# Output stage of a pooling trunk: P7 of five blocks as seven leaf products in place, row stores issued from GpSimd, operand work reordered

## The chip, the cores and the metric

One core of a Trainium2 chip runs the whole kernel. The metric is device time in microseconds (us) of that core. The kernel before takes 909.25 us, the median of three runs (909.12 to 909.44); the execution that the profiler recorded took 909.13 us, with a span of 907.3 us from its first to its last instruction. TensorE (PE in the profile) multiplies, VectorE (DVE) and ScalarE (ACT) do elementwise work and read results out of PSUM, GpSimd (POOL) does small elementwise work and issues some DMAs, SyncE (SP) issues most DMAs.

## The reference, cut to what matters

With one layer, the trunk is one pooling mixer between two RMSNorms:

```python
normed = rms_norm(x, norm_w[0])
u, gate = split(normed @ in_w, 2)            # 4096 x 1024 each
pooled = trailing means of u (windows 2, 4, 8, 16) - u
y = (einsum(pooled, group_w) + group_b) * scale * silu(gate)
h = x + y @ out_w                            # 4096x1024 @ 1024x1024
out = rms_norm(h, final_norm_w)
```

Everything is float32. The change touches the last two lines: the output product, the residual and the last norm.

## The kernel before, in words

**Products.** All large products follow Strassen's scheme in Winograd's form: seven products P1 to P7 of half-size matrices in place of eight. Each factor is held as a high and a low part in a float32 format that TensorE multiplies fast, and each half-size matmul is three passes: high·high, high·low, low·high (`mm3`, L774).

**Stages.** `steps` (L1287) lists the work in order: stages `a` and `b`, the input projection for four blocks of 1024 rows each, and then the output stage `o` for eight blocks (`NBO`) of 512 rows, `b` = 0 to 7. Within a block of the output stage the order is `ORDER_OUT` = P1, P7, P6, P2, P5, P4, P3 (L33). The main loop (L1566) goes through the steps `n`. At step `n` it issues loads for output steps up to `n + 4` (`load_o`, L1068), operand splits for up to `n + 2` (`split_o`, L1082), and then the products of step `n` with their eviction (`run`, L1322).

**A product of the output stage.** A block has four operand quarters 11, 21, 12, 22 of y, read from DRAM (`load_y`). `split_o` forms the sum that product needs and splits it: ScalarE copies it to the high part, VectorE subtracts to get the low part. The parts go to one of four operand tiles `op`, taken in turn. `product_out` (L894) runs two row halves `j`, each of four contraction chunks of three passes, 24 matmuls of 512 columns in all. The eight PSUM banks of 512 columns are four pairs x, v, y, spare, whose places turn from block to block (`sets_of`, L1315). P1 goes to x, and ScalarE copies it to y, so that P6 accumulates on it; P7 goes to v, P2 to x, P5 and P3 to y, P4 to v.

**Inner products.** In blocks 2 to 7, P2 is itself done as seven products of quarter-size matrices (`split_inner`, `product_inner`), here called leaves: two contraction chunks of three passes, six matmuls of 256 columns each. P2, P3, P4, P1, P7 run at P2's place; P6 and P5 within product P5; `add_inner` adds cells of the spare banks into rows with VectorE. The leaves' weights are formed in block 1 by `form_inner` into four kept tiles. A similar scheme in place, with cells of a bank copied to others between leaves, exists in stage `b` for two blocks (`product_seven`, L713); the output stage does not use it.

**Rows.** Output rows are collected in row tiles `hs` (two halves of a block, two tiles of 128 rows each). ScalarE evicts P7, P6 and P2 into them, GpSimd's accumulating DMAs add x (`add_h`, L1059), VectorE adds P5, P4, P3. `finish` (L1116) then normalizes a half, after P4 for the first and after P3 for the second: two squares of 1024 on ScalarE with their sums, a root on ScalarE (`inverse`, `rsqrt`), a reciprocal on VectorE refined by four small GpSimd operations, two row multiplies on VectorE, and two stores that SP issues. The junk output of a square goes to a tile from the common store. The last block has code of its own at its end (`late_factor`, `late_scalar`, `late_vector`).

**Tiles.** Operands, weights before splitting, rows and junk share 11 tiles `st` and 8 tiles `vt` (`Slots`, `take`, `give`, `keep`).

**Order.** A scheduler orders the instructions of each engine; `tc.issue_after(i)` makes what is issued inside come after instruction `i` in that order. Each engine then executes its own queue in that order, waiting on semaphores.

## Time and profile before

| | |
|---|---|
| median of three runs | 909.25 us |
| profiled execution, its own time | 909.13 us |
| its span | 907.3 us |
| busy: TensorE, VectorE, ScalarE, GpSimd | 898.9, 731.5, 494.0, 83.9 us |
| granted TensorE clock, mean over the span | 0.997 |
| first and last leaf of the output stage start | 701.0 and 889.6 us |

In the views below, a row of a timeline is: start in us from the start of the span, duration in us, engine, line, operation, tiles written and read, shape, count, and in brackets the idle time before it and what ended that. A row of a group ends with count, then busy us and mean ns of one, then idle time before with what ended it. A row of waits is: who waited for whom, us in total, times, longest. A row of windows is: the stretch, its length, then for each engine busy us and count, the granted clock, the busy share of the DMA engines, GB/s. A row of DMA issues ends with KB and the median us from issue to landing. Matmuls are pipelined, so a matmul's own duration (275 to 379 ns) is longer than the distance between starts; the distances are what counts.

### The profile page before, as it was taken

Reading aid. Unit: us, or ns where it says so; the run is one execution under the profiler, and the core shown is the slowest. Engines: PE = TensorE matmul, PEld = TensorE weight load, DVE = VectorE, ACT = ScalarE, POOL = GpSimd, SP = SyncE. Lnnn points to the kernel's source line nnn. Section 1 sums busy time; section 2 is a strip of 40 time slices with the busy share of each in tenths; the row PEclk is TensorE's granted clock in tenths of the full one; section 3 lists DMA queues with packets and bytes.
Section 4 is the critical chain, followed back from the end, with each engine's and each line's share of the span. In section 5 each row is a group of like instructions: output and inputs, shape, how many; then the busy total and the mean of one; then the engine's idle time right before and its main releaser. Section 6 shows DMA issues by size and latency. Waiting matters only on the chain.

```text
span 907.3 us, 11824 instructions
## 1 busy us (share of the span) xinstructions
PE 898.9 (99%) x4392; PEld 790.2 (87%) x4392; DVE 731.5 (81%) x868; ACT 494.0 (54%) x760; POOL 83.9 (9%) x166
## 2 busy tenths in 40 slices
PE   9999999999999999999999999999999999999996
PEld 7888888888888888889889888888888898988986
DVE  3889896985995999798599499599759768868686
ACT  7869547447446565346545636545535435445434
POOL 0020100100110000000000000001122113112200
PEclk9999999999999999999999999999999999999998
DMA  9987667677575462323554475528585675775732
GB/s 341 401 303 238 251 229 229 215 270 251 224 267 198 161 217 85 110 100 116 206 189 148 176 267 168 192 70 232 173 232 172 171 192 158 169 220 162 175 140 92
DMA packets 71401, 179.41 MB, mean 198 GB/s; under 512 B 6576, under 2 KB 24624, under 8 KB 71344
## 3 DMA queue, kind: packets, MB, share of 16 engines
q1 hardware_dynamic: 58720, 146.13, 46.4%
q0 software_dynamic: 11904, 31.48, 13.5%
q10 hardware_dynamic: 720, 1.06, 0.3%
q8 instruction: 34, 0.56, 0.3%
q14 instruction: 23, 0.19, 0.1%
HBM read 117.81 MB, written 60.83 MB: 197 GB/s over the span
## 4 chain that ended last, share of the span: by engine, by line
PE 95%; DVE 2%; DMA 1%; ACT 1%; issue 0%; DVEq 0%; ACTq 0%
PE bank L779 89%; PE bank L879 3%; PE bank L725 2%; PE bank L421 1%; DMA st<-in_x 1%; DMA early<-in_wut 0%; ACT st L461 0%; DVE vt L1245 0%; ACT st L1152 0%; PE bank L487 0%; DVE vt L172 0%; DVE w L169 0%; ACT st L443 0%; ACT early L443 0%; DVE vt L1204 0%
## 5 line engine op out<-in xcount | busy, mean ns | idle before, releaser
L779 PE MATMUL bank<-op,w 128*128 128x512 f32 x2592 | 560.9, 379 | 0.0
L779 PEld LDWEIGHTS bank<-op,w 128*128 128x128 f32 x2592 | 489.4, 189 | 70.2 <-ACT vt L175 0.4
L779 PE MATMUL bank<-w,op 128*128 128x512 f32 (+1 forms) x1212 | 262.2, 377 | 0.0
L779 PEld LDWEIGHTS bank<-w,op 128*128 128x128 f32 x1212 | 226.0, 189 | 31.0
L169 DVE TENSOR_TENSOR op<-st,op 128x1024 fp32r<-128x1024 f32 x134 | 162.3, 1219 | 58.0 <-ACT op L175 57.6
L175 ACT ACTIVATE op<-st 128x1024 fp32r<-128x1024 f32 x134 | 140.2, 1052 | 113.4 <-PE bank L779 64.5
L175 ACT ACTIVATE vt<-bank 128x512 f32<-128x512 f32 (+1 forms) x115 | 65.8, 590 | 46.5 <-PE bank L779 43.1
L169 DVE TENSOR_TENSOR st<-st,st 128x1024 f32<-128x1024 f32 (+1 forms) x42 | 45.8, 1104 | 18.9 <-ACT st L256 16.8
L169 DVE TENSOR_TENSOR op<-vt,op 128x1024 fp32r<-128x1024 f32 x42 | 51.1, 1219 | 8.1 <-ACT op L175 8.1
L175 ACT ACTIVATE op<-vt 128x1024 fp32r<-128x1024 f32 x42 | 44.1, 1054 | 24.9 <-PE bank L779 20.9
L1062 POOL DMA_DIRECT2D st<-in_x x19 | 16.8, 893 | 387.0 <-DVE op L169 352.9
L175 ACT ACTIVATE st<-bank 128x512 f32<-128x512 f32 (+1 forms) x61 | 34.7, 585 | 30.6 <-PE bank L779 19.1
L175 ACT ACTIVATE bank<-bank 128x512 f32<-128x512 f32 (+1 forms) x60 | 32.1, 537 | 30.1 <-PE bank L779 26.0
L933 DVE TENSOR_TENSOR_SCAN vt<-vt,window 128x1040 f32<-128x1040 f32 x16 | 37.9, 2376 | 1.6 <-DMA yd<-vt 1.5
L169 DVE TENSOR_TENSOR w<-st,w 128x1024 fp32r<-128x1024 f32 (+1 forms) x26 | 30.8, 1198 | 9.2 <-ACT w L175 9.2
L175 ACT ACTIVATE w<-st 128x1024 fp32r<-128x1024 f32 (+1 forms) x26 | 26.6, 1035 | 17.4 <-PE bank L779 9.5
L175 ACT ACTIVATE vt<-tails 128x32 f32<-128x32 f32 x28 | 6.3, 228 | 46.8 <-DVE vt L933 25.7
L979 DVE SCALAR_TENSOR_TENSOR vt<-vt,vt 128x1024 f32<-128x1024 f32 x24 | 29.3, 1219 | 0.3
L172 DVE TENSOR_TENSOR st<-st,vt 128x1024 f32<-128x1024 f32 x22 | 26.1, 1215 | 3.4 <-DMA vt<-rd 3.4
L1125 DVE SCALAR_TENSOR_TENSOR vt<-vt,ors,st 128x1024 f32<-128x1024 f32 x18 | 22.5, 1282 | 7.6 <-POOL ors L235 7.6
L1245 DVE TENSOR_TENSOR st<-bank,st 128x512 f32<-128x512 f32 x23 | 15.8, 689 | 14.0 <-PE bank L779 14.0
L984 DVE SCALAR_TENSOR_TENSOR st<-vt,colt,st 128x512 f32<-128x512 f32 x38 | 26.8, 743 | 0.1
(143 smaller groups left out, 735.3 us busy)
## 6 DMA issues: line engine op xcount, KB each, us to landing
st<-in_xt SPq DMA_DIRECT2D x28, 512.0 KB, 6.3
sd<-st POOLq DMA_DIRECT2D x28, 512.0 KB, 4.0
st<-sd SPq DMA_DIRECT2D x26, 512.0 KB, 4.2
st<-in_x SPq DMA_DIRECT2D x20, 512.0 KB, 6.0
st<-yd SPq DMA_DIRECT2D x20, 512.0 KB, 4.6
yd<-st SPq DMA_DIRECT2D x19, 512.0 KB, 3.1
out<-vt SPq DMA_DIRECT2D x18, 512.0 KB, 4.6
st<-wod SPq DMA_DIRECT2D x15, 512.0 KB, 4.0
```

The lines of the kernel that those rows point to most:

```text
L169: return nc.vector.tensor_tensor(out=dst, in0=a, in1=b, op=ALU.subtract)
L172: nc.vector.tensor_tensor(out=dst, in0=a, in1=b, op=ALU.mult)
L175: return nc.scalar.activation(dst, src, func)
L725: latest[0] = nc.tensor.matmul(cell(n, c).rearrange("p (a s) -> p a s", s=2), x1, x2, start=i == P1 and k + m == 0, stop=k == 1 and m == 2 ...
L779: latest[0] = nc.tensor.matmul(ps, a, b, start=start and n == 0, stop=stop and n == 2, skip_group_check=True).ins
L879: latest[0] = nc.tensor.matmul(ps, x1, x2, start=i in (P1, P7) and k + n == 0, stop=k == 1 and n == 2, skip_group_check=True,).ins
L933: nc.vector.tensor_tensor_scan(out=sums_[:, HIST:], data0=flat[:, HIST:], data1=flat[:, HIST - win : 2 * end - win], initial=first_sum, op ...
L979: nc.vector.scalar_tensor_tensor(out=s[:, :, at : at + H], in0=s[:, :, at : at + H], scalar=1.0 / win, in1=v[:, :, HIST:], op0=ALU.mult, o ...
L984: nc.vector.scalar_tensor_tensor(out=sg[:, j], in0=s[:, j, at : at + H], scalar=bias_c[2 * grp + j], in1=sg[:, j], op0=ALU.add, op1=ALU.mult,)
L1062: nc.gpsimd.dma_start(out=hs[b][half, j][:, n], in_=x[row_of(b, half, j), n * H : (n + 1) * H], accum_op=ALU.add,)
L1125: nc.vector.scalar_tensor_tensor(out=us[j], in0=us[j], scalar=rs[:, j : j + 1], in1=fw[0], op0=ALU.mult, op1=ALU.mult,)
L1245: partial["added"] = nc.vector.tensor_tensor(out=dst, in0=src, in1=dst, op=ALU.add).ins
```

## The change

- Blocks from 3 on (`OWN` = 3, five blocks) do P7 as seven leaves in place in the pair v. The first two leaves (P1 and P5) are put into the last quarter of product P1 (`own_first`); the others are put around P6's first row half, of which six matmuls each stand between leaves (`own_rest`). Four copies of 256 columns on ScalarE (`own_move`) take cells of the banks to other cells or to a row tile between leaves, and one VectorE add completes the second bank.
- The operand of P7 is split as P2's is: four narrow sums of 256 columns, and two operand tiles (`split_own`).
- The weights of the leaves are formed in block 1 for P2 and in block 2 for P7 (`load_inner`, `sum_inner`, `split_weight`), with three kept tiles each. Sums are formed in place in the loaded tiles.
- P2's leaves at its place run in the order P2, P4, P1, P3, P7, and the split of its four sums is issued later than that of its plain quarters (`late_split`).
- `finish` squares the two halves of a row apart (512 each), with the junk output in a PSUM bank, and GpSimd adds the two sums before the root. Row multiplies and stores of a block's first half are issued after the narrow sums of the next block's P7, where that is done by leaves (`late_rows`). Stores are issued by GpSimd.
- Row tiles are taken when P1 and P2 of the block run, not four steps ahead (blocks 0 to 6).
- Operand work of step `n + 2` is ordered behind the reading out of the products of step `n - 2` (`read_out`).

```diff
+OWN = 3
...
+    def load_inner(i):
+        raws[i] = {"held": [take() for _ in range(2)]}
+        for h, u in enumerate(raws[i]["held"]):
+            nc.sync.dma_start(out=u, in_=wod[i][h])
+
+    def sum_inner(i):
+        us = raws[i]["held"]
+        b11, b12 = (quarter(us[0], j) for j in range(2))
+        b21, b22 = (quarter(us[1], j) for j in range(2))
+        if i == P7:
+            sub(b12, b11, b12)
+            sub(b22, b22, b12)
+            add(b11, b22, b11)
+            sub(b21, b21, b22)
...
+    def split_weight(i, *ps):
+        for p in ps:
...
+            copy(home[0], raws[i][p])
+            sub(home[1], raws[i][p], home[0].bitcast(F32))
...
+    def split_own(u):
+        at = u.rearrange("p (g k) (j c) -> p g j k c", g=2, j=2)
+        b11, b12, b21, b22 = (at[:, g, j] for g in range(2) for j in range(2))
+        v = take("p (n k c) -> p n k c", n=4, k=2)
+        sub(v[:, 0], b12, b11)
+        sub(v[:, 1], b22, v[:, 0])
+        sub(v[:, 2], b22, b12)
+        row_sums[0] = sub(v[:, 3], b21, v[:, 1]).ins
+        plain_op = next_op("p (s g k j c) -> p s g j k c", s=2, g=2, k=2, j=2)
+        split(plain_op.rearrange("p s g j k c -> p s (g k) (j c)"), u)
+        sums_op = next_op("p (s n k c) -> p s n k c", s=2, n=4, k=2)
+        split(sums_op, v)
...
+    def own_move(dst, src):
+        with tc.issue_after(own.get("moved", latest_copy[0])):
+            own["moved"] = copy(own["m5"] if dst is None else own_cell(dst), own_cell(src)).ins
+
+    def own_first(t, b, sets):
+        own.clear()
+        own.update(t=t, v=sets["v"])
+        own_into(P1, 1, True)
+        own_into(P5, 3)
...
+        own_move(0, 1)
+        own_move(None, 3)
+
+    def own_rest(piece):
+        own_into(P2, 0)
+        own_into(P6, 1)
+        own_move(2, 1)
+        piece(0)
+        own_into(P7, 2)
+        own_into(P3, 1)
+        own_move(3, 2)
+        piece(1)
+        own_into(P4, 2)
+        bank = own["v"][1].rearrange("p (j b) -> p j b", j=2)
+        add(bank, bank, own["m5"].unsqueeze(1).to_broadcast([P, 2, 256]))
...
-            for p in (P2, P3, P4, P1, P7):
+            for p in (P2, P4, P1, P3, P7):
                 product_inner(p)
...
-    def finish(b, half):
+    def finish(b, half, sets):
+        parts = small.tile([P, 2, 2], F32, tag="parts", name=f"parts{b}_{half}")
...
-            junk = take("p (a b) -> p a b", a=2)
-            nc.scalar.activation(junk, us[j], AF.Square, accum_out=ss[:, j : j + 1])
-            give(junk)
+            for n in range(2):
+                nc.scalar.activation(
+                    sets["v" if half else "y"][j], us[j][:, n], AF.Square,
+                    accum_out=parts[:, n, j : j + 1],
+                )
+        nc.gpsimd.tensor_tensor(out=ss, in0=parts[:, 0], in1=parts[:, 1], op=ALU.add)
         rs = inverse(b, half, ss)
+        if half and b + 1 >= OWN:
+            late_rows.append(lambda: norm_rows(b, half, us, rs))
+        else:
+            norm_rows(b, half, us, rs)
...
-            nc.sync.dma_start(
+            nc.gpsimd.dma_start(
                 out=out[row_of(b, half, j), :], in_=us[j].rearrange("p a b -> p (a b)")
             )
...
+        if kind == "o" and b < NBO - 1 and i in (P1, P2):
+            load_h(b, int(i == P1))
+        if kind == "o" and b >= OWN and i == P1:
+            t = split_up.pop(n)
+            out_part(P1, t, sets["x"][0], 0, range(4))
+            out_part(P1, t, sets["x"][1], 1, range(2))
+            own_first(split_up.pop(n + 1), b, sets)
+            with tc.issue_after(latest[0]):
+                out_part(P1, t, sets["x"][1], 1, range(2, 4))
+            evict_o(b, i, sets)
...
+        (1, P1): lambda: load_inner(P2),
+        (1, P6): lambda: sum_inner(P2),
+        (1, P5): lambda: split_weight(P2, P7, P6),
+        (1, P4): lambda: (split_weight(P2, P5, P4), end_weights(P2)),
+        (2, P1): lambda: load_inner(P7),
+        (2, P6): lambda: sum_inner(P7),
+        (2, P5): lambda: split_weight(P7, P7, P6),
+        (2, P4): lambda: (split_weight(P7, P5, P3), end_weights(P7)),
...
-        advance("split", n, split_step, split_reach)
...
+        if kind == "o" and i == P6 and late_split:
+            with tc.issue_after(own["moved"]) if own else nullcontext():
+                late_split.pop()()
+        with ExitStack() as order:
+            for ins in read_out.get(n - 2, {}).values():
+                order.enter_context(tc.issue_after(ins))
+            advance("split", n, split_step, split_reach)
+        for f in late_rows:
+            with tc.issue_after(row_sums[0]):
+                f()
+        late_rows.clear()
```

200 lines of the change are left out of this document (122 added, 78 removed).

## The prediction

> **What bounds the kernel now.** I read the page first (busy shares, the chain that ended last), then TensorE in order of time over two blocks of the output stage, then what TensorE ever waited for.
>
> ```profile
> span 907.3 us, 11824 instructions
> ...
> PE 95%; DVE 2%; DMA 1%; ACT 1%; issue 0%; DVEq 0%; ACTq 0%
> ```
> ```profile
> 710.89 26.07 PE L779 MATMUL bank<-w,op 128*128 128x512 f32 x120
> 736.79 1.50 PE L879 MATMUL bank<-w,op 128*128 128x256 f32 x12
> 738.13 0.83 PE L879 MATMUL bank<-inner,op 128*128 128x256 f32 x6
> 738.80 0.83 PE L879 MATMUL bank<-w,op 128*128 128x256 f32 x6
> ...
> 740.14 2.75 PE L779 MATMUL bank<-w,op 128*128 128x512 f32 x12
> ...
> 746.66 13.55 PE L779 MATMUL bank<-w,op 128*128 128x512 f32 x62
> ```
> ```profile
> PE bank L1374 <- PEq L1685: 0.8, 1, 0.8
> PE bank L421 <- DMA early<-in_group_w: 0.4, 1, 0.4
> ```
>
> TensorE holds 95% of the chain, and its only two waits lie in the first microseconds. Starts give the prices: 120 matmuls of 512 columns take 736.79 − 710.89 = 25.90 us, 215.8 ns each; thirty leaf matmuls of 256 columns take 740.14 − 736.79 = 3.35 us, 111.7 ns each; a leaf of six takes 0.67. So a plain output product (24 × 215.8) costs 5.18 us and seven leaves (42 × 111.7) cost 4.69. A block of six plain products and one of leaves is 6 × 5.18 + 4.69 = 35.77 us without a gap. Only two things can move the end: less work on TensorE, or a wait put in front of it.
>
> **The change on TensorE.** In blocks 3 to 7, P7 becomes seven leaves: 5 × (5.18 − 4.69) = 2.45 us less. That is the whole gain, 0.27%. P2's leaves only change order, and everything up to the output stage keeps its order on each engine.
>
> The Trainium skill ("TensorE: Matmul & The Clock Gate", Back-to-back issue gap) gives N/2.4 + 2.5 ns for one matmul after another; 512 columns agree with the 215.8, 256 columns would be 109.2 against the measured 111.7, and the gain by it would be 2.97 us. The same section's sustained figure of about 131 ns for 512 columns is not what this trace shows; the row decides.
>
> ```profile
> L175 ACT ACTIVATE op<-st 128x1024 fp32r<-128x1024 f32 x43 | 45.1, 1056 | 64.5 <-PE bank L779 40.5 <-DVE st L169 10.8 <-PE bank L879 7.8
> ```
>
> **The work added, and its cover.** Per block from 3 on: one more operand split of 1024 (ScalarE 1.06, VectorE 1.22 us), four narrow sums instead of none (0.42 each), four bank moves of 256 columns, one add of 512 (0.69, as a bank add below); and everywhere eight squares of 512 into a PSUM bank in place of four of 1024, and a GpSimd add in front of each root.
>
> ```profile
> 720.70:756.50 35.80, 35.80 (x188) 31.94 (x187) 24.09 (x32) 15.85 (x25) 7.54 (x15) 1.00 0.66 169
> 756.50:792.30 35.80, 35.80 (x188) 31.94 (x187) 30.64 (x41) 18.33 (x27) 9.54 (x17) 1.00 0.70 183
> ```
>
> These windows (TensorE, weight load, VectorE, ScalarE, GpSimd) are a block long each. VectorE is busy 24 to 31 us of 35.8, ScalarE 16 to 18. By the durations above the change adds 1.22 + 4 × 0.42 + 0.69 = 3.6 us of VectorE per block, so the sum still fits, some 85% full; in block 2 it must also form the weights of P7's leaves (four sums and four low parts of 512, 8 × 0.69 = 5.5 us), which all but fills the block. The two 512 KB loads for them and the later loads of the row tiles have a block or more of lead. As a mean all this hides behind TensorE. The edits that only hold work back (the split of P2's sums, operand work behind an older product's reading out, the row multiplies behind P7's narrow sums) cost nothing of their own; they set the order in which all this stands in front of one wait.
>
> **The new wait.** In-place leaves need results moved between cells while the product runs. Set t = 0 where P1 starts on TensorE. It does 18 matmuls of P1, leaves P1 and P5, the last six of P1: 24 × 0.2158 + 2 × 0.67 = 6.52 us. Then leaf P2 accumulates onto a copy of cell 1, made by ScalarE. In the built program that move does not stand early in ScalarE's queue: ahead of it are the four squares of the previous block's second row half, the copy of P1's first bank, and (blocks 4 to 7) the root, which now waits for the GpSimd add of the squares' halves. The last two squares wait for VectorE's add of P3's second half, and that stands on VectorE behind the previous half's two row multiplies, which wait for GpSimd's reciprocal-root refinement. Before, no matmul waited for any of this.
>
> ```profile
> 749.45 0.69 DVE L1245 TENSOR_TENSOR st<-bank,st 128x512 f32<-128x512 f32 x1 [0.39 <-PE bank L779]
> ...
> 753.15 1.22 DVE L166 TENSOR_TENSOR vt<-vt,vt 128x1024 f32<-128x1024 f32 x1
> 754.28 1.22 DVE L169 TENSOR_TENSOR op<-st,op 128x1024 fp32r<-128x1024 f32 x1
> 755.42 0.16 DVE L220 RECIPROCAL ors<-otmp 128x2 f32<-128x2 f32 x1
> 755.50 0.67 DVE L1245 TENSOR_TENSOR vt<-bank,vt 128x512 f32<-128x512 f32 x1
> 756.78 1.28 DVE L1125 SCALAR_TENSOR_TENSOR st<-st,ors,st 128x1024 f32<-128x1024 f32 x1 [0.62 <-POOL ors L235]
> 757.99 1.28 DVE L1125 SCALAR_TENSOR_TENSOR vt<-vt,ors,st 128x1024 f32<-128x1024 f32 x1
> 759.18 0.68 DVE L1245 TENSOR_TENSOR vt<-bank,vt 128x512 f32<-128x512 f32 x1
> ...
> 760.92 0.42 DVE L169 TENSOR_TENSOR st<-vt 128x256 f32<-128x256 f32 x1
> 761.25 1.22 DVE L169 TENSOR_TENSOR op<-vt,op 128x1024 fp32r<-128x1024 f32 x1
> ```
>
> VectorE in order of time, block 3 to 4 of before. The last leaf ends at 746.66, so P4 runs from there, P3 from 751.84, and t = 0 is 757.02. P4's first half is added at 749.45 (t = −7.57) and P3's second half at 759.18 (t = +2.2). Start to start a 1024 operation takes 1.13 us, a row multiply 1.21, a bank add 0.6 to 0.67, a narrow sum 0.33 (its full 0.42 when the next one needs it), and the row multiplies begin 1.36 after the reciprocal. Blocks 4 to 7 of the new kernel hold from t = −7.57: add 0.65, three narrow sums 1.1, a low part 1.13, add 0.6, narrow sum 0.35, a sum 1.13, a dependent one 1.2, a low part 1.13: reciprocal at −0.28. Row multiplies from 1.08 to 3.50, P3's second half added by 4.2, two microseconds later than before.
>
> ```profile
> 890.66 0.63 ACT L1152 ACTIVATE st<-vt 128x512 f32<-128x512 f32 x1 [6.96 <-DVE vt L889]
> 891.19 0.19 ACT L1152 ACTIVATION_READ_ACCUMULATOR st<-vt 128x1 f32 x1
> 891.41 0.63 ACT L1152 ACTIVATE st<-vt 128x512 f32<-128x512 f32 x1
> ```
> ```profile
> 724.35 0.29 ACT L216 ACTIVATE otmp<-oss,eps 128x2 f32<-128x2 f32 x1
> 724.55 0.58 ACT L175 ACTIVATE bank<-bank 128x512 f32<-128x512 f32 x1
> ```
> ```profile
> L175 ACT ACTIVATE bank<-bank 128x256 f32<-128x256 f32 x12 | 4.4, 370 | 4.0 <-PE bank L725 4.0
> ```
> ```profile
> 764.64 1.22 DVE L169 TENSOR_TENSOR vt<-vt,st 128x1024 f32<-128x1024 f32 x1
> 764.78 1.13 POOL L217 TENSOR_SCALAR oms<-oss 128x2 f32<-128x2 f32 x1 [8.04 <-ACT st L1121]
> ```
> ```profile
> L217 POOL TENSOR_SCALAR oms<-oss 128x2 f32<-128x2 f32 x14 | 6.9, 491 | 83.8 <-ACT st L1121 46.5 <-ACT vt L1121 37.2
> ```
>
> Two squares of 512 at 0.75 each end at 5.75; GpSimd's add (nearest row: its small multiply, 0.19 alone, 1.13 at worst, 0.49 in the mean) at best near 6.0; the root 0.2 and the move 0.37 give 6.6; three or four hand-overs of 0.1 make it 6.9 (an estimate: the add at 749.45 starts 0.2 after its matmuls). TensorE wanted 6.52: 0.4 us late, 1.3 with the worst GpSimd add. I take the mean of that row, 0.3 above its floor: 0.7 us a block, 2.8 us for blocks 4 to 7. After it the chain starts anew from P4 of the block, so the stall is paid each time and not carried on.
>
> The 1.13 us multiply ends with the VectorE operation that it met (764.64 + 1.22). The Trainium skill ("SBUF — State Buffer", Who interferes with whom) says the same: a VectorE operation with two SBUF inputs locks the port that a GpSimd read needs for its whole length. Were each GpSimd step of the chain so blocked, a block would lose the 1.3 us and the whole run 2.4 us more than I take.
>
> Block 3 has another order: ahead of its move stand P3's squares, the copy of P1's bank and also P6's operand copy of 1.06 us, and VectorE comes out of the full block 2 at about t = −5.9 instead of −7.57 (the extra narrow leaf adds, two low parts of the new weights, P1's low part). From there 0.65, two leaf adds 0.8, 0.6, 0.33, 1.13, 0.33, 1.13: reciprocal at −0.9, row multiplies from 0.5 (free GpSimd) or 1.5 (blocked) for 2.4, then P3's two adds: 3.55 to 4.55 for the first. ScalarE then holds square 0.75, bank copy 0.58, squares 0.75 + 0.75, operand copy 1.06, square 0.75, move 0.37, 5.0 in all, or 4.8 since start to start is some 0.1 shorter than an operation's length: 8.4 to 9.4, 1.9 to 2.9 late. I take the middle, 2.4.
>
> Later moves have room: the second is 0.3 us behind the first while leaf P2 takes 0.67; the third has the 1.3 us of six P6 matmuls to cover one operand copy and one move; the fourth likewise. P7's eviction, now beside P6, ends near t = 15; P5's operand is still ready a microsecond before its 19.
>
> ```profile
> vt<-in_x POOLq DMA_DIRECT2D x23, 256.0 KB, 5.4
> out<-vt SPq DMA_DIRECT2D x18, 512.0 KB, 4.6
> L1062 POOL DMA_DIRECT2D vt<-in_x x23 | 20.3, 927 | 60.2 <-DVE vt L889 32.1 <-ACT vt L175 19.0 <-ACT op L175 8.3
> ```
>
> Stores through GpSimd: four a block at 0.93 of issue, each waiting for its row multiply, ahead of that half's GpSimd add and of the four accumulating loads of x. The first pair issues at t = 2.4 to 4.6, clear of the add at 5.75; the second lets the loads issue from about 14 and land 5.4 later, near 20 to 22, where P5's first add (21.6) reads them. On SP the loads no longer stand behind stores. I book nothing; without that cover VectorE waits up to a microsecond there, and leaf P5, due at 24.9, has two to spare.
>
> Sum: page run 907.3 of span and 909.13 in all, with 1.83 outside it that I leave; −2.45 + 2.8 + 2.4 = +2.75, so 911.9; the median before is 0.12 above that run: **912.0 us**.
>
> **Rivals.** A: the moves are in time. My walk is late by 0.4 in its best case, of which the hand-overs are the whole; if VectorE runs 0.5 us ahead of my addition in every block and block 2 keeps up, no wait is left: 909.25 − 2.45 = 906.8. For it: ScalarE and VectorE have idle time in both windows. Against it: the chain is serial and idle time elsewhere doesn't shorten it. B: only block 3 stalls: 906.8 + 2.4 = 909.2. C: the GpSimd queue decides. If each of the stores or small adds in the chain is held behind VectorE operations as at 764.78, or block 2's VectorE falls further behind and P6's and P2's operands come late too, blocks 4 to 7 lose 1.3 and block 3 some 4: 906.8 + 5.2 + 4 = 916.
>
> **How the numbers follow.** Forecast 0.60 (its own range 910.2 to 914.5, from 0.4 and 1.9 late, to 1.2 and 2.9), A 0.20, B 0.08, C 0.12. About 0.2% (1.8 us) can be told from no change, so 911.07 and 907.43 are the bounds: of the forecast's 0.60 about 0.13 lies under 911.07. Slower 0.47 + 0.12 = 0.59; same 0.13 + 0.08 = 0.21; faster 0.20. The range goes from A's 906.7 to 914.8.
>
> **What would show it.** In the profile after: TensorE pauses in blocks 3 to 7 right before the second group of P7's leaves, 6.5 us after P1 starts, released by a 128x256 bank move on ScalarE; block 3's pause two to three times the others'; the root ahead of that move waiting for GpSimd; P3's second add about 4 us after P1's start. P7's leaves at 0.67 each confirm the gain. Wrong would be blocks of 35.3 us without a pause (A), or a pause before another product: P5, P1 or P6 released by an operand (C).

## The result, and the profile after

| | us |
|---|---|
| before, median of 4 runs beside it | 909.35 (909.12 to 909.69) |
| after, median of 4 runs | 921.91 (920.29 to 923.71) |
| ratio | 1.0138, 95% interval 1.0119 to 1.0158 |
| profiled execution of after, its own time | 922.18, span 920.4, mean granted clock 0.995 |

The change makes the kernel slower by 12.6 us. 912.0 was forecast with a range of 906.7 to 914.8: the side was right, the size was not.

The page of after, the shares of the chain that ended last:

```profile
PE 79%; DVE 8%; DMA 5%; issue 4%; ACT 2%; POOL 1%; SPq 0%; DVEq 0%; POOLq 0%; ACTq 0%
```

TensorE held 95% of the chain and now holds 79%. VectorE, DMA and "issue" (time for which the profile shows no wait) stand in it instead. What TensorE waited for in the output stage (waits of TensorE from 700 us on: in total, times, longest):

```profile
PE bank L920 <- DVE st L981: 4.6, 2, 3.2
PE bank L920 <- ACT bank L176: 3.5, 4, 2.2
PE bank L920 <- DVE vt L981: 1.5, 1, 1.5
```

And TensorE in order of time, each leaf that began late (L920 is the leaf, L780 a matmul of 512 columns; the bracket holds the idle time and what ended it):

```profile
730.52 1.65 PE L920 MATMUL bank<-w,op 128*128 128x256 f32 x6 [2.24 <-ACT bank L176]
731.96 1.49 PE L920 MATMUL bank<-inner,op 128*128 128x256 f32 x6
733.24 1.82 PE L780 MATMUL bank<-w,op 128*128 128x512 f32 x6
734.90 1.50 PE L920 MATMUL bank<-inner,op 128*128 128x256 f32 x12
...
768.01 0.94 PE L920 MATMUL bank<-w,op 128*128 128x256 f32 x6 [0.31 <-ACT bank L176]
823.21 0.94 PE L920 MATMUL bank<-w,op 128*128 128x256 f32 x6 [1.35 <-DVE st L981]
841.68 0.94 PE L920 MATMUL bank<-w,op 128*128 128x256 f32 x6 [0.65 <-ACT bank L176]
862.91 0.98 PE L920 MATMUL bank<-w,op 128*128 128x256 f32 x6 [3.23 <-DVE st L981]
863.69 16.09 PE L780 MATMUL bank<-w,op 128*128 128x512 f32 x66
898.75 0.94 PE L920 MATMUL bank<-inner,op 128*128 128x256 f32 x6 [1.48 <-DVE vt L981]
```

Three kinds of loss lie here.

- **Leaf P2 of product P7 waits for ScalarE's move** (released by L176) in blocks 3 to 6. Start to start the delay is 2.42, 0.48, 0.48 and 0.82 us, 4.2 in all (the idle time and some 0.17 more, by which a matmul's end in these rows lies behind the place where the next one could start). Block 5's row is as block 4's, at 803.87.
- **Leaf P5, in product P5, waits for VectorE's adds of an inner bank** (L981) in blocks 5 and 6, and leaf P6 does in block 7: 1.51, 3.40, 1.72 and a smaller one of 0.19, 6.8 in all.
- **TensorE is slow after two of these pauses**, those of 2.24 and 3.23 us. Behind 730.52 the two leaves take 1.44 and 1.28 us from start to start instead of 0.67, and the six matmuls behind them 1.66 instead of 1.30: 1.75 us. The 66 matmuls behind 863.69 are shown as 16.09 us; the same row has 14.41 in blocks 3 and 5 of this execution: 1.68 us.

The granted clock (third column from the right in the windows, which have the busy time of TensorE, weight load, VectorE, ScalarE and GpSimd ahead of it) shows why:

```profile
728.00:732.00 4.00, 1.76 (x9) 1.48 (x8) 2.79 (x6) 3.54 (x11) 1.16 (x4) 0.82 0.59 197
...
864.00:868.00 4.00, 4.00 (x13) 3.18 (x13) 3.17 (x5) 1.88 (x2) 1.66 (x2) 0.62 0.03 8
```

The sum from the first leaf of block 2 (701.02 before, 701.36 after) to the last matmul: −2.45 + 4.2 + 6.8 + 3.4 + 0.7 = +12.7. The 0.7 are seven leaves behind a pause that take 0.77 us from start to start in place of 0.67.

Why is VectorE late at L981? Its adds stand behind the adds of P5 into the rows (L1360). VectorE's longest waits from 700 us on; then rows of block 6 in order of time (SPq is a DMA that SP issues, L1141 a load of y, L1148 one of x, L1158 an accumulating load of x, L780 here the first row half of P5); then GpSimd's first three loads with the time from issue to landing:

```profile
DVE vt L1360 <- DMA vt<-in_x: 15.0, 4, 6.5
```
```profile
849.15 0.38 SPq L1141 DMA_DIRECT2D st<-yd  x1
849.39 0.90 POOL L1158 DMA_DIRECT2D st<-in_x  x1 [3.09 <-ACT st L176]
849.63 0.45 SPq L1141 DMA_DIRECT2D vt<-yd  x1
850.03 1.20 POOL L1158 DMA_DIRECT2D vt<-in_x  x1
850.60 1.54 POOL L1158 DMA_DIRECT2D vt<-in_x  x1
852.19 0.34 SPq L1148 DMA_DIRECT2D vt<-in_x  x1
853.66 2.76 PE L780 MATMUL bank<-w,op 128*128 128x512 f32 x12
...
861.83 0.69 DVE L1360 TENSOR_TENSOR vt<-bank,vt 128x512 f32<-128x512 f32 x1 [6.47 <-DMA vt<-in_x]
```
```profile
st<-in_x POOLq DMA_DIRECT2D x1, 256.0 KB, 7.7
vt<-in_x POOLq DMA_DIRECT2D x1, 256.0 KB, 9.1
vt<-in_x POOLq DMA_DIRECT2D x1, 256.0 KB, 11.1
```

ScalarE has evicted P7 by then, and the loads leave one behind the other. VectorE is idle from 855.36 (861.83 − 6.47), and the matmuls that it reads end at 856.42 (853.66 + 2.76). The data come 5.3 us later: the add starts 0.1 us after the third load has landed (850.60 + 11.1 = 861.7), so that one, the last of the three to leave, brings the x that it reads. The x of P7's other row half left first, and x for P6 second.

### The profile page after: what moved, and what is told of

Read it like the earlier page. It is cut to its first block, busy times and chain, and to the rows that moved or that the text cites. A ratio compares the mean times of both kernels' runs of the same rounds, so it can differ in the third digit from the quotient of the medians.

```text
span 920.4 us, 12164 instructions
## 1 busy us (share of the span) xinstructions
PE 901.5 (98%) x4482; PEld 793.4 (86%) x4482; DVE 750.0 (81%) x908; ACT 513.3 (56%) x847; POOL 107.7 (12%) x208
## 4 chain that ended last, share of the span: by engine, by line
PE 79%; DVE 8%; DMA 5%; issue 4%; ACT 2%; POOL 1%; SPq 0%; DVEq 0%; POOLq 0%; ACTq 0%
PE bank L780 74%; PE bank L920 2%; DMA vt<-in_x 2%; PE bank L726 2%; DVE op L170 2%; DVE vt L170 2%; DMA early<-in_wut 1%; DMA st<-in_x 1%; DVE vt L1360 1%; PE bank L422 1%; ACT bank L1227 1%; DVE st L1360 1%; DVE st L1240 0%; DVE vt L1240 0%; DMA early<-in_group_w 0%
## 5 line engine op out<-in xcount | busy, mean ns | idle before, releaser
L780 PE MATMUL bank<-op,w 128*128 128x512 f32 x2592 | 560.7, 379 | 0.0
L780 PEld LDWEIGHTS bank<-op,w 128*128 128x128 f32 x2592 | 489.5, 189 | 69.9 <-ACT bank L176 0.4
L780 PE MATMUL bank<-w,op 128*128 128x512 f32 (+1 forms) x1092 | 241.7, 379 | 0.0
L780 PEld LDWEIGHTS bank<-w,op 128*128 128x128 f32 x1092 | 203.4, 191 | 27.4 <-issue 0.2
L170 DVE TENSOR_TENSOR op<-st,op 128x1024 fp32r<-128x1024 f32 x125 | 151.5, 1219 | 56.0 <-ACT op L176 55.5
L176 ACT ACTIVATE op<-st 128x1024 fp32r<-128x1024 f32 x125 | 130.7, 1051 | 54.9 <-PE bank L780 30.4
L176 ACT ACTIVATE vt<-bank 128x512 f32<-128x512 f32 (+1 forms) x128 | 72.2, 583 | 55.0 <-PE bank L780 55.0
L176 ACT ACTIVATE op<-vt 128x1024 fp32r<-128x1024 f32 x56 | 58.5, 1052 | 64.6 <-PE bank L920 29.5
L1158 POOL DMA_DIRECT2D vt<-in_x x31 | 28.5, 1052 | 412.9 <-DVE vt L1029 352.8
L170 DVE TENSOR_TENSOR op<-vt,op 128x1024 fp32r<-128x1024 f32 x56 | 68.0, 1218 | 9.6 <-ACT op L176 9.4
L176 ACT ACTIVATE bank<-bank 128x512 f32<-128x512 f32 (+1 forms) x75 | 37.7, 504 | 41.9 <-PE bank L780 25.5
L176 ACT ACTIVATE st<-bank 128x512 f32<-128x512 f32 (+1 forms) x53 | 30.3, 589 | 32.6 <-PE bank L780 17.9
L920 PEld LDWEIGHTS bank<-w,op 128*128 128x128 f32 x264 | 34.2, 194 | 11.8 <-ACT bank L176 5.4
L920 PE MATMUL bank<-w,op 128*128 128x256 f32 x264 | 36.3, 281 | 8.1 <-DVE st L981 4.6
L1360 DVE TENSOR_TENSOR vt<-bank,vt 128x512 f32<-128x512 f32 x37 | 25.2, 684 | 21.8 <-DMA vt<-in_x 15.0
L1227 ACT ACTIVATE bank<-vt 128x512 f32<-128x512 f32 x42 | 25.1, 597 | 20.7 <-DVE vt L1360 20.2
L176 ACT ACTIVATE w<-st 128x1024 fp32r<-128x1024 f32 (+1 forms) x26 | 26.6, 1035 | 16.9 <-PE bank L780 10.7
L176 ACT ACTIVATE vt<-tails 128x32 f32<-128x32 f32 x28 | 6.3, 228 | 43.7 <-DVE vt L1029 24.5
```

The lines of the kernel that those rows point to most:

```text
L170: return nc.vector.tensor_tensor(out=dst, in0=a, in1=b, op=ALU.subtract)
L176: return nc.scalar.activation(dst, src, func)
L780: latest[0] = nc.tensor.matmul(ps, a, b, start=start and n == 0, stop=stop and n == 2, skip_group_check=True).ins
L920: latest[0] = nc.tensor.matmul(ps, x1, x2, start=start and k + n == 0, stop=k == 1 and n == 2, skip_group_check=True,).ins
L1158: nc.gpsimd.dma_start(out=hs[b][half, j][:, n], in_=x[row_of(b, half, j), n * H : (n + 1) * H], accum_op=ALU.add,)
L1227: nc.scalar.activation(sets["v" if half else "y"][j], us[j][:, n], AF.Square, accum_out=parts[:, n, j : j + 1],)
```

## The experiments

The ratio stands against runs of the kernel before on the same chip. "Output differs" marks a kernel whose output is not the reference's, because it leaves work out or reads what it has overwritten.

| run | median us | ratio, 95% interval |
|---|---|---|
| stores through SP | 919.27 | 1.0102 (1.0087 to 1.0117) |
| no x for P7's rows (output differs) | 915.17 | 1.0054 (1.0039 to 1.0070) |
| P7 plain (output differs) | 909.59 | 0.9999 (0.9990 to 1.0008) |
| squares behind two moves | 916.74 | 1.0073 (1.0056 to 1.0090) |
| x loaded straight | 914.96 | 1.0058 (1.0043 to 1.0074) |
| squares behind three moves | 914.88 | 1.0058 (1.0043 to 1.0073) |
| both | 910.69 | 1.0013 (1.0004 to 1.0022) |
| both, stores through SP | 910.70 | 1.0013 (1.0003 to 1.0022) |
| four blocks, root behind the moves | 912.04 | 1.0026 (1.0016 to 1.0036) |
| five blocks, root behind the moves | 916.94 | 1.0085 (1.0071 to 1.0099) |
| rows later | 910.47 | 1.0013 (1.0003 to 1.0022) |
| rows later, one subtraction later | 910.72 | 1.0016 (1.0007 to 1.0025) |
| fewer stores (output differs) | 923.03 | 1.0141 (1.0123 to 1.0158) |
| block 7 relieved | 911.27 | 1.0017 (1.0008 to 1.0026) |
| block 7 relieved, one subtraction later | 909.19 | 0.9996 (0.9987 to 1.0005) |
| small y (output differs) | 918.73 | 1.0101 (1.0087 to 1.0115) |
| last rows later | 908.80 | 0.9993 (0.9984 to 1.0002) |

### Which part of the change costs

**P7 plain in every block, all other edits kept.**

```diff
-OWN = 3
+OWN = 8
```

> Changed kernel with P7 a plain product in every block, all other edits kept (stores through GpSimd, stored weights formed for P7 too, hold of the operand work, late add of x). Theory: all the loss comes from the leaves of P7 and what they move, so this is 909.3 us, within 0.6. Rival (the other edits cost by themselves, stores through GpSimd first): leaf P5 still waits, 912 to 917 us.

909.59: as before. Stores through GpSimd, the hold of operand work, the squares in halves and the weights of P7's leaves (formed though not used; the plain P7 reads a weight of which one quarter they have overwritten, so its output differs) cost nothing by themselves. All the loss needs P7 as leaves. Block 6 here, in order of time:

```profile
840.73 0.90 POOL L1158 DMA_DIRECT2D vt<-in_x  x1 [1.37 <-ACT vt L176]
...
850.03 0.69 DVE L1360 TENSOR_TENSOR vt<-bank,vt 128x512 f32<-128x512 f32 x1 [1.40 <-PE bank L780]
```

With P7 plain, 9.3 us lie between the first load of x, here the one for P5's first add, and that add, which waits for TensorE and not for data. With leaves, 856.42 − 850.60 = 5.8 us lie between the load and the time when TensorE has the product: P7 is complete only after the matmuls of P6 that stand between its leaves, and this load leaves third. (The late row multiplies go with the leaves, and fall away here too.)

**Stores through SP.**

```diff
-            nc.gpsimd.dma_start(
+            nc.sync.dma_start(
                 out=out[row_of(b, half, j), :], in_=us[j].rearrange("p a b -> p (a b)")
```

> Changed kernel with one edit undone: the normalised rows are stored through SP again, not through GpSimd. Theory Q (the stores stand ahead of the x loads in GpSimd's queue, so x comes late and leaf P5 waits): the leaf P5 waits of blocks 5 to 7 (6.6 us) and the slow clock behind the one of block 6 (1.7 us) go, 921.9 - 8.3 = 913.6 us. Theory L (x is late because product P7, now seven products, is evicted some 4 us later, and the loads meet the loads of y): leaf P5 waits stay, 921 to 923 us.

919.27, between the two. The waits of blocks 5 and 6 stay (1.66 and 3.39 idle), that of block 7 goes, and in the profiled execution block 3 kept its clock after its pause of 2.24. So the stores on GpSimd's queue are not what makes x late in blocks 5 and 6; that the stores' place matters for block 7 was not followed further.

**No x for P7's rows**, in blocks 3 to 6; this part of the sum is left out.

```diff
-        if not final and i in (P7, P6):
+        if not final and (i == P6 or i == P7 and b < OWN):
             add_h(b, half, n)
```

> Changed kernel in which blocks 3 to 6 do not add x to the quarter of rows that P7 fills (this part of the sum is left out). If leaf P5 waits only because VectorE's adds of P5 wait for this x: its waits (1.5, 3.4, 1.7, 0.2 = 6.8 us) and the slow clock after block 6's (1.7 us) go, 921.9 - 8.5 = 913.4 us (912.5 to 914.5). If VectorE is late for another reason too (it has more work before P5): the waits shrink to less than half at the most, above 917 us.

915.17 (913.11 to 916.26), 6.7 us less than after, where 8.5 was expected, block 7's wait among them. TensorE's waits of this run, from 700 us on:

```profile
PE bank L920 <- ACT bank L176: 3.2, 4, 2.2
PE bank L920 <- DVE vt L981: 1.5, 1, 1.5
```

The waits of blocks 5 and 6 are gone and leaf P2's stay, as the theory has it. Block 7's stays too, so it is not this x that holds it.

**x loaded straight**: the same, with nothing left out.

```diff
-            elif half == 0:
+            elif half == 0 or b >= OWN:
                 nc.sync.dma_start(out=u[:, 1], in_=x[row_of(b, half, j), H:])
...
-            if not final and i in (P7, P6, P2):
+            if not final and (i in (P6, P2) or i == P7 and b < OWN):
                 seen["scalar"] = copy(halved(u), plain(ps[j])).ins
```

(`add_h` for P7 goes as above; P7's rows then fall to VectorE's add.)

> Changed kernel in which, for blocks 3 to 6, SP loads x straight into the quarter of rows that P7 fills, ahead of time, and VectorE adds P7's banks to it (two adds of 0.7 us a block in place of two ScalarE copies and two accumulating loads). Nothing is left out. Theory: the late x alone holds VectorE before leaf P5, so this stands where the run without that x stood, 915.2 us (914 to 917); leaf P2 waits stay. Rival: VectorE's 1.4 us more, in its fullest stretch, bring the leaf P5 waits back: above 918 us.

914.96, where the run without x stood, and the same waits (3.2 for the move, 1.5 in block 7). VectorE had room for the two adds. The late x is worth 7 us.

### Why the move is late

**Squares behind two moves.**

```diff
-            finish(b, 1 if i == P4 else 0, sets)
+            if i == P3 and b + 1 >= OWN:
+                late_squares.append((b, 0, sets))
+            else:
+                finish(b, 1 if i == P4 else 0, sets)
...
         own_move(None, 3)
+        with tc.issue_after(own["moved"]):
+            for args in late_squares:
+                finish(*args)
+        late_squares.clear()
```

> Changed kernel in which ScalarE's squares and root of the upper half of a block (finish after P3) are queued behind the two moves of the next block's P7 for blocks 3 to 7. If leaf P2 waits only for these squares: 4.2 us of waits, the 1.75 us of slow clock in block 3 and 0.4 us of restarts go, 921.9 - 6.3 = 915.6 us (914.5 to 917). If the moves then wait for something else (the banks, the operand copies): above 918 us. Leaf P5 waits should be as before or up to 2 us longer, since the products come earlier against the x loads.

916.74. Leaf P2's wait is gone in blocks 4 to 7, so it was those squares and the root, but each block has a new wait two leaves on. Block 4 (ScalarE's L1231 is a square):

```profile
766.38 0.61 ACT L1231 ACTIVATE bank<-vt 128x512 f32<-128x512 f32 x1
...
770.47 0.37 ACT L176 ACTIVATE bank<-bank 128x256 f32<-128x256 f32 x1
```
```profile
770.90 1.60 PE L920 MATMUL bank<-inner,op 128*128 128x256 f32 x12 [1.17 <-ACT bank L176]
```

The third move, at 770.47, now stands behind the four squares.

No leaf P5 waits here, though its waits were expected to stay or grow: the 916.74 lies in the range that the theory gave by another sum. Block 6 shows why. TensorE runs from the last of P7's leaves to P5 at the same times as in after, to 0.01 us, and y's loads go out beside x as there (849.21 to 850.63). But the three loads of x leave GpSimd in another order:

```profile
849.76 0.90 POOL L1162 DMA_DIRECT2D vt<-in_x  x1 [1.88 <-ACT vt L176]
850.33 1.26 POOL L1162 DMA_DIRECT2D st<-in_x  x1
850.95 1.55 POOL L1162 DMA_DIRECT2D vt<-in_x  x1
...
857.96 0.69 DVE L1364 TENSOR_TENSOR vt<-bank,vt 128x512 f32<-128x512 f32 x1 [2.87 <-DMA vt<-in_x]
```

The x of P5's first add is now the first of the three. It lands 8.1 us after its issue, at 857.9; in after, as the third, it lands at 861.7. VectorE still waits for it, but not long enough to hold leaf P5. The order of the loads is the order in which ScalarE evicts the row halves. No run changed it alone.

**Squares behind three moves**, and in block 3 the split of P6's operand behind the first two moves. The `late_squares` loop stands in `own_rest` behind `own_move(2, 1)`, and:

```diff
-        return 2 if kind == "o" and (b, i) != (0, P1) else 1
+        return 2 if kind == "o" and (b, i) not in ((0, P1), (OWN, P6)) else 1
...
             own_first(split_up.pop(n + 1), b, sets)
+            if b == OWN:
+                at["split"] += 1
+                with tc.issue_after(own["moved"]):
+                    split_step(at["split"])
```

> Changed kernel in which ScalarE's squares and root of the upper half are queued behind the third move (2,1) of the next block's P7, and in block 3 the split of P6's operand behind the first two moves; x comes as in the changed kernel. Theory: no leaf waits for a move or a bank, so block 3 to 7 keep only the leaf P5 waits, which come back in full since nothing holds the products up ahead of them: 909.7 - 2.45 + 6.8 + 1.7 = 915.8 us (913 to 917). Rival (x was late because of the stores, which now come later too): no leaf P5 waits, 907 to 909 us.

914.88, in the range that the theory gave, but not with the waits that it named: no leaf P5 waits, and operands are late instead. Block 5, in order of time:

```profile
808.84 1.54 POOL L1162 DMA_DIRECT2D vt<-in_x  x1
815.15 0.69 DVE L1364 TENSOR_TENSOR vt<-bank,vt 128x512 f32<-128x512 f32 x1 [1.43 <-DMA vt<-in_x]
816.62 13.63 SPq L1145 DMA_DIRECT2D vt<-yd  x3
823.13 1.23 DVE L170 TENSOR_TENSOR vt<-vt,vt 128x1024 f32<-128x1024 f32 x1 [4.93 <-DMA vt<-yd]
838.92 1.13 PE L780 MATMUL bank<-w,op 128*128 128x512 f32 x4 [1.72 <-DVE op L170]
```

Rows stored later give their tiles back later, so two loads of y go out at 816.6 and not beside x. x lands 6.2 us after its issue at 808.84, and now y is late and holds VectorE 4.9 us. What one transfer gains the other loses.

**Both** (this and x loaded straight), and **both with stores through SP**.

> The two edits together: squares behind the third move, x loaded straight by SP and P7 added by VectorE. Theory (leaf P2 waits, leaf P5 waits and the slow clock after them are the whole loss): 909.7 - 2.45 = 907.3 us, 906.5 to 908.5, faster than before by 0.1 to 0.35%. If the change costs something else: above 910 us.

> As the two edits together, and the rows stored through SP again. Theory: nothing waits for the stores, so as with the two edits, 906.5 to 908.5 us, the last product's leaf in block 7 (1.7 us, seen with stores on GpSimd only) gone if it was still there. Rival: SP's loads of y stand behind the stores, as before the change, and come late: 1 to 4 us more than the run with the two edits alone.

910.69 and 910.70, above the 906.5 to 908.5 that was expected of both. The waits of after are gone; 3.4 us over the sum of 907.3 remain, and where the stores are issued makes no difference. TensorE's blocks 5 and 6 start 35.64 us apart here (797.31 to 832.95), 0.36 over the forecast's 35.28: the leaf P3 of product P2 waits 0.3 for its operand's low part on VectorE.

### Why x lands late

**Fewer stores**: the lower half's rows of blocks 2 to 6 are not stored.

```diff
+            if not half or b + 1 < OWN:
                 nc.gpsimd.dma_start(
                     out=out[row_of(b, half, j), :], in_=us[j].rearrange("p a b -> p (a b)")
                 )
```

> Changed kernel that leaves out the stores of the lower half's rows of blocks 2 to 6 (2 x 512 KB a block; those rows of the output are not written). The x loads are issued when P7 is evicted, as in the changed kernel. Theory C (x lands late because it shares the DMA engines with y loads that come bunched, when the stored rows' tiles come free): the y loads come earlier, x lands sooner, leaf P5's waits (6.8 us) and the slow clock after them fall to a third or less, 921.9 - 6 = 916 us, 914 to 918. Theory L (P7's later eviction alone leaves too little time for the accumulating loads): the waits stay, 920 to 922 us.

923.03, a little above the 920 to 922 of theory L: the waits stay (2.04 and 3.14 idle in blocks 5 and 6). The y loads still went out beside x (849.69, 851.19 and 851.67, with x at 851.41), so this excludes the left-out stores as the cause and says nothing on the y loads.

**Small y**: y's lower half of blocks 4 to 7 is loaded with a quarter of its bytes; the rest of the tile keeps what it held.

```diff
-        nc.sync.dma_start(out=u, in_=yd[b][:, 4 * kh : 4 * kh + 4, t : t + TH])
+        m = 1 if b > OWN and half else 4
+        nc.sync.dma_start(out=u[:, 0:m], in_=yd[b][:, 4 * kh : 4 * kh + m, t : t + TH])
```

> Changed kernel in which the loads of y's lower half for blocks 4 to 7 (two of the four 512 KB loads a block, those that go out beside the x loads) bring a quarter of their bytes (the rest of the tile keeps what it held, so the output of these blocks differs). Theory C (x lands late because it shares the DMA engines with those loads): x lands sooner, leaf P5's waits (6.8 us) fall below 2 us, 921.9 - 6 = 916 us, 914.5 to 918. Theory L (P7's later eviction alone leaves too little time): the waits stay, 920 to 923 us.

918.73, between the two theories. VectorE's adds of P5 in blocks 5 and 6, in order of time:

```profile
820.30 0.69 DVE L1361 TENSOR_TENSOR vt<-bank,vt 128x512 f32<-128x512 f32 x1 [3.43 <-DMA vt<-in_x]
...
858.93 0.69 DVE L1361 TENSOR_TENSOR vt<-bank,vt 128x512 f32<-128x512 f32 x1 [5.40 <-DMA vt<-in_x]
```

From issue to landing the x of these adds takes 8.1 and 10.1 us here, against 9.3 and 11.1 in after. The idle time before the leaves falls from 6.1 to 3.0. So both theories hold a part: the load has 3.5 us less time than with P7 plain (9.3 − 5.8, 1.2 of it because it leaves last of three), and it shares the DMA engines with more. The two 512 KB loads of x for block 7, beside it in block 6, were not taken away.

A third part is the order of the three loads, which no theory named. The time from issue to landing of the x that P5's first add reads:

| run | its place among the three | block 5, us | block 6, us |
|---|---|---|---|
| after | third | 9.3 | 11.1 |
| small y | third | 8.1 | 10.1 |
| squares behind three moves (two loads of y come later) | third | 6.2 | 7.4 |
| squares behind two moves | first | 6.9 | 8.1 |

### What is left, and whether the change can pay

**Four and five blocks, the root behind the moves.** x loaded straight; only the root, not the squares, behind the first two moves. With four blocks `OWN` = 4 and the weights are formed a block later; with five blocks P6's operand in block 3 is split behind the moves, as above.

```diff
-        rs = inverse(b, half, ss)
...
+        def root():
+            rs = inverse(b, half, ss)
...
+        if not half and b + 1 >= OWN:
+            late_roots.append(root)
+        else:
+            root()
```

> P7 as seven products in blocks 4 to 7 only (its weights formed one block later), x loaded straight by SP and P7 added by VectorE, and ScalarE's root of the upper half (not its squares) queued behind the first two moves. Theory: no leaf P2 wait is left and block 3's (2.4 us and its slow clock) does not arise, gain 4 x 0.49 = 1.96 us, what remains is the wait of block 7's leaf P6 for VectorE (1.5 us): 909.5 - 2.0 + 1.6 = 909.1 us, 907.5 to 910; without that wait 907.5. Rival (VectorE, with three us more work a block, is late elsewhere too): 910 to 912 us.

> As the run with four blocks, but with blocks 3 to 7, and in block 3 the split of P6's operand queued behind the two moves. Theory: block 3's first move stands behind VectorE's last add of block 2 and its squares only, 0.3 to 0.8 us of wait in place of 2.4, block 7's wait for VectorE stays: 909.5 - 2.45 + 0.6 + 1.6 = 909.3 us, 908 to 910.5. Rival (the move of block 3 still comes 2 us late): 911 to 912 us.

912.04 and 916.94, both misses. Past the first block with leaves no move is waited for, and blocks start 35.28 us apart, the forecast's block to the hundredth. With five blocks, the first two leaves of blocks 5, 6 and 7 start at 802.50, 837.78 and 873.06. The loss sits in the first block (3.24 us idle with four blocks; 1.45 for the move and 3.38 for P6's operand with five, where splitting it behind the moves was the wrong cure) and in block 7. VectorE where the first block begins, with four blocks (L1251 is a row multiply, L1371 P3's adds):

```profile
761.01 1.28 DVE L1251 SCALAR_TENSOR_TENSOR st<-st,ors,st 128x1024 f32<-128x1024 f32 x1
762.22 1.28 DVE L1251 SCALAR_TENSOR_TENSOR vt<-vt,ors,st 128x1024 f32<-128x1024 f32 x1
763.41 1.28 DVE L1371 TENSOR_TENSOR vt<-bank,vt 128x512 f32<-128x512 f32 x2
```

P3's two adds, for which the squares wait, stand behind both row multiplies.

**Rows later**: these two multiplies behind P3's adds and the subtraction for P6's operand, with five blocks and P6's split where the change has it. **One subtraction later**: also P3's operand in block 7 is formed a step later.

```diff
-        for f in late_rows:
-            with tc.issue_after(row_sums[0]):
-                f()
-        late_rows.clear()
+        if kind != "o" or (b + 1, i) != (OWN, P3):
+            for f in late_rows:
+                with tc.issue_after(row_sums[0]):
+                    f()
+            late_rows.clear()
...
-        return 2 if kind == "o" and (b, i) != (0, P1) else 1
+        return 2 if kind == "o" and (b, i) not in ((0, P1), (NBO - 1, P3)) else 1
```

> As the run with four blocks (x straight by SP, the root behind the moves), but with blocks 3 to 7, and where the first of them begins, VectorE multiplies the two lower rows of block 2 behind the last two adds of P3 and the subtraction for P6's operand, not ahead of them. Theory: in the runs before, those two multiplications of 1.24 us, put ahead, held the adds, so the squares, so the moves of the first block; leaf P2's wait there falls from 2.3 or 3.2 us to under 0.5, and only block 7's leaf P6 waits (1 to 1.5 us): 909.3 - 2.45 + 0.3 + 1.6 = 908.8 us, 908 to 909.6. Rival (the first block's moves are late for another reason): 911 us or more.

> The same, and in block 7 the subtraction for P3's operand (VectorE, 1.2 us) is queued behind the first add of an inner bank. Theory: leaf P6 of block 7 then waits 0.3 us in place of 1.5: 909.3 - 2.45 + 0.3 + 0.5 = 907.6 us, 907 to 908.5, faster than before by 0.1 to 0.25%. Rival (VectorE is full there, and P3's operand is now late): as the run without it, 908.8 us or more.

910.47 and 910.72, both above the ranges that were expected (908 to 909.6 and 907 to 908.5). In the first, the first block's wait for a move is gone (the theory's step), and TensorE has three waits in all, one of 0.42 in block 3 and these:

```profile
882.25 2.83 PE L780 MATMUL bank<-w,op 128*128 128x512 f32 x12 [0.63 <-DVE st L1371]
886.55 0.94 PE L920 MATMUL bank<-inner,op 128*128 128x256 f32 x6 [1.48 <-DVE st L985]
```

These two, 2.1 us idle, are in block 7, where VectorE adds every product into rows that x already fills. Moving one subtraction alone only moves them (0.88, 0.47, 0.64), a miss.

**Block 7 relieved**: P6 by ScalarE copies and accumulating loads of x there too, and then with the subtraction later.

```diff
-            if not final and (i in (P6, P2) or i == P7 and b < OWN):
+            if i == P6 or not final and (i == P2 or i == P7 and b < OWN):
                 seen["scalar"] = copy(halved(u), plain(ps[j])).ins
```

> As the run with rows later (blocks 3 to 7), and in block 7 P6 is evicted by two ScalarE copies and x added by GpSimd's accumulating loads, as in the other blocks, in place of two VectorE adds of 0.7 us. Theory (the 2.4 us lost in block 7 are VectorE's, whose work there runs without a gap): its waits for P5's adds and leaf P6 fall by 1 to 1.4 us, 910.5 - 1.3 = 909.2 us. Rival (the waits hang on one product's eviction that comes later anyway): 910 to 911 us.

> The same, and the subtraction for P3's operand of block 7 behind the first add of an inner bank. Theory: the wait of leaf P6 of block 7 goes too, 908.2 us, 907.3 to 909, faster than before by up to 0.2%. Rival: as the run without it, or 910 to 911 us.

911.27 and 909.19, where 909.2 and 908.2 were expected. Alone the relief merges two waits into one of 2.34, and the clock drops behind it (its leaf shown as 1.65); with the subtraction later 0.25 and 0.35 are left. The two edits are worth something only together.

**Last rows later**: on top of that, the two row multiplies of block 6's upper half behind P5's adds in block 7.

```diff
-            else:
-                norm_rows(b, half, us, rs)
+            elif not half and b == NBO - 2:
+                last_rows.append(lambda: norm_rows(b, half, us, rs))
+            else:
+                norm_rows(b, half, us, rs)
```

> As the run with VectorE relieved in block 7 and the subtraction later (909.2 us), and the two row multiplications of block 6's upper half (2.5 us of VectorE) behind P5's adds in block 7. Theory: VectorE's lateness in block 7 goes (0.6 us of waits and their restarts), 909.2 - 0.9 = 908.3 us, faster than before by 0.1%. Rival: the 2.5 us fall into the last adds and multiplications, and the tail behind the last matmul grows, 910 to 911.5 us.

908.80 against 909.50 beside it, ratio 0.9993 (0.9984 to 1.0002): not told from no change. One wait is left in blocks 2 to 7, of 0.41 in block 3. The last long group:

```profile
888.29 10.61 PE L780 MATMUL bank<-w,op 128*128 128x512 f32 x60
```

From the first leaf at 701.34 to the start of this group TensorE takes 186.95 us, against 188.72 before (701.02 to 889.74) and a forecast of 188.72 − 2.45 = 186.27. But the tail behind the last matmuls, 907.1 − 898.9 = 8.2 us, is 1.2 longer than before (907.3 − 900.35 = 6.95), and 0.9 longer than without this last edit (907.4 − 900.1 = 7.3): the rival of this run was right in part. 1.8 gained, 1.2 given back.

## Why the prediction came out as it did

- **The gain, −2.45: right.** Seven leaves in place of a product; blocks without a wait are 35.28 us apart, as worked out.
- **Leaf P2 in block 3, +2.4: right in place and chain, and in size with some luck** (2.42). The rows of ScalarE are the ones named, in the order named:

```profile
726.18 0.60 ACT L1227 ACTIVATE bank<-vt 128x512 f32<-128x512 f32 x1 [4.46 <-DVE vt L1360]
726.81 0.58 ACT L176 ACTIVATE bank<-bank 128x512 f32<-128x512 f32 x1
727.33 0.58 ACT L1227 ACTIVATE bank<-vt 128x512 f32<-128x512 f32 x1
727.93 0.58 ACT L1227 ACTIVATE bank<-vt 128x512 f32<-128x512 f32 x1
728.54 1.04 ACT L176 ACTIVATE op<-vt 128x1024 fp32r<-128x1024 f32 x1
729.49 0.58 ACT L1227 ACTIVATE bank<-vt 128x512 f32<-128x512 f32 x1
730.10 0.36 ACT L176 ACTIVATE bank<-bank 128x256 f32<-128x256 f32 x1
```

  P1 starts at 725.48 − 3.88 = 721.60, so the first square starts at t = 4.6, the late end of the 3.55 to 4.55 that the walk gave. The squares take 0.6 us and not 0.75, so the chain is 4.3 us long (726.18 to 730.46) and not 4.8. The two errors cancel.

- **Leaf P2 in blocks 4 to 7, +2.8: right mechanism, too large.** 0.48, 0.48, 0.82 and 0, so 1.8. The walk's best case was 0.4, and I added 0.3 for GpSimd's small add over its floor of 0.19; it took 0.38 in blocks 4 to 6 and 0.19 in block 7. In block 7 the first move ends at 882.2, just as TensorE comes to it.
- **The stores and the loads of x, "I book nothing": this is the step that failed.** It is worth 4.9 us of delay before leaf P5 in blocks 5 and 6 and 1.7 of slow clock behind it, 6.6 in all; two runs that take this x away measured 6.7 and 7.0. The sentence had x issued from t = 14 and landed 5.4 later, near 20 to 22, where P5's first add (21.6) reads it. In block 6 (P1 starts 838.23 − 3.88 = 834.35) the three loads left at t = 15.0 to 16.2, which is little. The matmuls of that add were done at t = 22.1, near the forecast. But its x left last of the three and landed at t = 27.4, after 11.1 us in place of 5.4. The 5.4 was a median of before; the run with P7 plain shows what lead these loads have there, 9.3 us. The edit moved the loads among those of y, shortened the lead to 5.8 and changed their order. "VectorE waits up to a microsecond" was 5.4 (856.42 to 861.83), and "leaf P5 has two to spare" was spent.
- **Block 7, 1.9 us: not in the sum either.** This delay stays when P7's x is left out, so it is not that step's. Waits of 0.25 and 0.35 are left when two edits together move VectorE's work there (909.19).
- **The clock: not in the sum at all.** A pause of more than two microseconds was priced at its own length; two of them cost 1.7 us more each.
- **Rivals.** A (no wait, 906.8) is what the last run shows TensorE can nearly do, with six edits more. B is out. C priced the loss at 9.2 us, where 15.1 came (12.7 + 2.45), and the stated range ended at 914.8, below C's own 916. Its causes do not fit: with the stores moved back to SP the waits before leaf P5 in blocks 5 and 6 are still there, and in after no matmul of the output stage waits for an operand.

Settled: the late x is worth 7 us (two runs); with x loaded straight, the squares and block 3's operand split behind the moves are worth 4.3 more (914.96 to 910.69); and nothing else in the change costs by itself. Not settled: how the shorter lead, the company of other transfers and the order of the three loads share in x's lateness. The order is read from two runs that differ in more than it, where x lands some 3.8 us sooner in block 6 (857.9 against 861.7); a run that puts the load for P5's first add ahead of the others was not made. Not settled either: why block 7 waited less with stores on SP.

## What to carry to other kernels

When an edit makes a product finish later, follow what is issued by its eviction: a transfer that was hidden had a lead, and the lead is what to compare with its landing time under the load of that moment, not with a median. Where several transfers leave together, look which one is needed first: here it left last. Price a pause of TensorE beyond 2 us with the slow stretch that can follow it. A product made shorter pays only if the engines that feed its inner steps have slack at that point: here each cure moved the wait to the next queue, until the last block and the tail behind it had taken most of the gain.

## What the runs showed of the hardware

- **The granted clock can fall after a pause of TensorE of 2.24 us.** In the profiled executions, all five pauses of 3.14 to 3.39 us were followed by a window of 4 us at 0.57 to 0.68; of nine pauses of 2.04 to 2.34 us, three were (2.24 in after, 2.25 with fewer stores, 2.34 with block 7 relieved) and six were not, among them 2.24 with stores through SP, and 2.25 with x left out and with x straight; no pause under 2 us was. Leaves take about twice their time then (1.44 and 1.28 us in place of 0.67), and each of the two pauses of after lost 1.7 us more. The Trainium skill ("TensorE: Matmul & The Clock Gate", What's actually happening) has the clock halve after an idle window of about 3.4 us that runs freely: chance at the same length of pause agrees with a free-running window, but here two thirds of that length was enough.
- **An accumulating load of 256 KB took 5.4 us (median of those into `vt` tiles, before) to 11.1 us from issue to landing**, by what else was under way; with two of the loads beside it cut to a quarter it was about 1.1 us less.
- **Accumulating loads that GpSimd issued one behind the other landed one behind the other.** In block 6 of after three left within 1.2 us (849.39, 850.03, 850.60) and landed after 7.7, 9.1 and 11.1 us.
